# Row-wise infinity norm of an 8192 x 8192 matrix: a tiled load-and-reduce loop replaced by a ring with hand-placed semaphores, 64 KB runs, a shrinking tail and a split first load

## The chip, the cores and the metric

The kernel runs on one core of one Trainium2 chip. The metric is the device time of one execution in microseconds (us); the program is one launch, with its input and its output in the chip's main memory.

## The reference

For every row of `x`, the largest absolute value in the row:

```
x: float32, 8192 rows x 8192 columns
out[i] = max over j of |x[i, j]|          # np.linalg.norm(x, ord=np.inf, axis=1)
```

So 268.44 MB are read, and 8192 numbers (32 KB) are written. There is no reuse of data.

## The kernel before

The 8192 rows are cut into T = 64 tiles of 128 rows; row p of a tile lies in partition p. One tile is 128 x 8192 float32, 4 MB, and one partition's share of it is one run of 32 KB of memory.

A single loop runs over the 64 tiles. For each tile a buffer of a pool of five (`pool`, `bufs=5`) is taken, and the tile is loaded and reduced in pieces of columns. The list `chunks` gives the pieces: 54 tiles have one piece of 8192 columns; the last ten follow the list `COOLDOWN`: seven of 4096 + 4096, then 4096 + 2048 + 2048, then four times 2048, then 2048, 2048, 1536, 1280 and 1280. For each piece:

- L55 issues the load from SyncE (SP), the only engine that issues loads. SP's program is a plain list, so the loads enter its DMA queue in the order of the loop. A load of a tile whose buffer was in use waits, on SP, for the reduce that read that buffer five tiles before.
- L59 reduces the piece on VectorE (DVE) along the columns with `max` of absolute values. For a tile of one piece the result goes to column t of `res` (128 x 64), else to a column of `partial`.
- For a tile of several pieces, L68 then reduces the few columns of `partial` to column t of `res`. It has to wait for the reduce just before it on the same engine.

After the loop, L78 transposes `res` on TensorE (PE) with an identity matrix that GpSimd (POOL) made at the start, L80 copies the 64 x 128 result from PSUM to SBUF on VectorE, and L81 stores it from SP, 64 rows of 512 B. The tile framework places all semaphores. It ends with a barrier of all engines, a clearing of semaphores and a second barrier.

So the order of the work is: SP's list of loads, held back only by free buffers; VectorE's list of reduces, held back by landings; and a last chain of transpose, copy, store and barriers after the last reduce.

Of the kernel before, what the change touches and what calls it, by code (L numbers as in the profile page):

```python
# [1 line left out]

# [5 lines left out]


COOLDOWN = (
    [[4096, 4096]] * 7
    + [[4096, 2048, 2048]]
    + [[2048, 2048, 2048, 2048]]
    + [[2048, 2048, 1536, 1280, 1280]]
)


@with_exitstack
def kernel(  # L20
    ctx: ExitStack,
    tc: tile.TileContext,
    x: bass.AP,
    out: bass.AP,
):
    nc = tc.nc
    P = 128
    n_rows, n_cols = x.shape
    assert n_rows % P == 0

    T = n_rows // P
    if n_cols == 8192 and T >= len(COOLDOWN):
        chunks = [[n_cols]] * (T - len(COOLDOWN)) + COOLDOWN
    else:
        chunks = [[n_cols]] * T

    x_t = x.rearrange("(t p) m -> t p m", p=P)

    pool = ctx.enter_context(tc.tile_pool(name="sbuf", bufs=5))
    single = ctx.enter_context(tc.tile_pool(name="single", bufs=1))  # L40
    psum_pool = ctx.enter_context(tc.tile_pool(name="psum", bufs=1, space=bass.MemoryType.PSUM))

    res = single.tile([P, T], mybir.dt.float32)
    maxch = max(len(c) for c in chunks)
    if maxch > 1:
        partial = single.tile([P, maxch], mybir.dt.float32)

    for t in range(T):
        ch = chunks[t]
        assert sum(ch) == n_cols  # L50
        xt = pool.tile([P, n_cols], x.dtype)
        off = 0
        for h, w in enumerate(ch):
            dst = res[:, t : t + 1] if len(ch) == 1 else partial[:, h : h + 1]
            nc.sync.dma_start(  # L55
                out=xt[:, off : off + w],
                in_=x_t[t, :, off : off + w],
            )
            nc.vector.tensor_reduce(  # L59
                out=dst,  # L60
                in_=xt[:, off : off + w],
                axis=mybir.AxisListType.X,
                op=mybir.AluOpType.max,
                apply_absolute_value=True,
            )
            off += w
        if len(ch) > 1:
            nc.vector.tensor_reduce(  # L68
                out=res[:, t : t + 1],
                in_=partial[:, : len(ch)],  # L70
                axis=mybir.AxisListType.X,
                op=mybir.AluOpType.max,
            )

    ident = single.tile([P, P], mybir.dt.float32)
    make_identity(nc, ident)
    res_t_psum = psum_pool.tile([T, P], mybir.dt.float32)
    nc.tensor.transpose(res_t_psum, res, ident)  # L78
    res_t = single.tile([T, P], mybir.dt.float32)
    nc.vector.tensor_copy(out=res_t, in_=res_t_psum)  # L80
    nc.sync.dma_start(out=out.rearrange("(t p) -> t p", p=P), in_=res_t)  # L81


# [1 line left out]
_INS = ['x']  # L85
_OUTS = [((8192,), 'float32')]


# [23 lines left out]
```

## Time and profile before

| What | Value |
|---|---|
| time, median of 3 runs | 634.72 us (634.71 to 634.74) |
| the profiled execution's own time | not listed apart from the three |
| span of the profiled execution, first to last instruction | 632.9 us |
| VectorE busy | 558.9 us, 88%, 91 instructions |
| PE busy | 0.4 us |
| GpSimd busy | 0.7 us |
| input loads | 80, in one DMA queue |
| reduces of 8192 columns (L59) | 54, mean 8686 ns |
| reduces of 4096 / 2048 columns (L59) | 15 at 4416 ns / 8 at 2278 ns |
| second reduce of a cut tile (L68) | 10, mean 156 ns |
| PE transpose (L78), copy (L80) | 393 ns, 283 ns |
| issue of a full load to its landing, median | 39.8 us |
| store of the result, issue to landing | 1.8 us |

How to read the profile: the page cuts the span into 40 slices of 15.8 us. The DMA row is the mean busy share of the core's 16 DMA engines in each slice, in tenths, and the GB/s row is what they moved. The chain that ended last is followed back from the last instruction, at each step to what released it. A line of the timeline gives the start in us, the length in us, the engine, the source line, the operation with output<-input, the shapes, how many instructions are merged in it, and in brackets the idle time before it and what ended that. A line of the window table gives a stretch in us, its length, the busy time of PE, PE's weight load, VectorE and GpSimd with numbers of instructions, the granted clock, the DMA engines' busy share and the GB/s they moved.

### The profile page before, as it was taken

How to read it: one execution, taken by the hardware profiler on the slowest of the kernel's cores; microseconds unless marked ns; L12 is line 12 of the kernel's file. 1: busy time of each engine (PE TensorE's matmuls, PEld its weight loads, DVE VectorE, ACT ScalarE, POOL GpSimd, SP SyncE). 2: the span in 40 equal slices, each digit the busy share in tenths (PEclk: the TensorE clock that was granted, in tenths of full speed). 3: DMA queues.
4: the chain of work that ended last, by engine and by line, in shares of the span. 5: the costliest groups of instructions: out<-in, count | busy, mean ns of one | idle time of the engine just before them, and what ended most of it. 6: DMA issues, size and time to landing. Idle time of an engine off the chain costs nothing.

```text
span 632.9 us, 294 instructions
## 1 busy us (share of the span) xinstructions
PE 0.4 (0%) x1; PEld 0.1 (0%) x1; DVE 558.9 (88%) x91; POOL 0.7 (0%) x6
## 2 busy tenths in 40 slices
PE   0000000000000000000000000000000000000000
PEld 0000000000000000000000000000000000000000
DVE  1988988988989889889898898898988989999997
POOL 0000000000000000000000000000000000000000
DMA  8999999999999999999999999999999999999995
GB/s 373 439 437 437 433 431 433 431 431 431 431 431 431 431 431 431 431 431 431 431 431 431 431 431 431 431 431 431 431 437 433 435 435 418 427 428 431 425 421 219
DMA packets 11602, 268.49 MB, mean 424 GB/s; under 512 B 1296, under 2 KB 1360, under 8 KB 1744
## 3 DMA queue, kind: packets, MB, share of 16 engines
q1 hardware_dynamic: 11600, 268.47, 98.9%
q14 instruction: 2, 0.02, 0.0%
HBM read 268.44 MB, written 0.03 MB: 424 GB/s over the span
## 4 chain that ended last, share of the span: by engine, by line
DMA 75%; DVE 24%; SPq 0%; issue 0%; PE 0%; DVEq 0%
DMA xt<-in_x_dram 75%; DVE res L59 15%; DVE partial L59 8%; SPq L55 0%; DVE res L68 0%; PE res_t_psum L78 0%; DVE res_t L80 0%; DVEq L59 0%
## 5 line engine op out<-in xcount | busy, mean ns | idle before, releaser
L59 DVE TENSOR_REDUCE res<-xt 128x1 f32<-128x8192 f32 x54 | 469.0, 8686 | 67.6 <-DMA xt<-in_x_dram 67.6
L59 DVE TENSOR_REDUCE partial<-xt 128x1 f32<-128x4096 f32 (+3 forms) x26 | 88.1, 3430 | 2.7 <-DMA xt<-in_x_dram 2.6
L68 DVE TENSOR_REDUCE res<-partial 128x1 f32<-128x2 f32 (+3 forms) x10 | 1.6, 156 | 0.3
L80 DVE COPY res_t<-res_t_psum 64x128 f32<-64x128 f32 x1 | 0.3, 283 | 0.6 <-PE res_t_psum L78 0.6
L78 PE MATMUL res_t_psum<-ident,res 128*64 128x128 f32 x1 | 0.4, 393 | 629.5 <-DVE res L68 629.5
masks.py:199 POOL TENSOR_SCALAR_AFFINE_SELECT ident<-ident 128x128 f32<-128x128 f32 x1 | 0.3, 292 | 0.1
L78 PEld LDWEIGHTS res_t_psum<-ident,res 128*64 128x64 f32 x1 | 0.1, 128 | 629.4 <-issue 629.4
masks.py:197 POOL MEMSET ident<- 128x128 f32 x1 | 0.2, 204 | 0.3 <-POOLq L96 0.3
L96 POOL MEMSET const-bfloat16-1.0<- 128x1 bf16 x1 | 0.1, 101 | 0.0
L96 POOL MEMSET const-uint8-127<- 128x1 uint8 x1 | 0.1, 101 | 0.0
L96 POOL MEMSET const-float32-0.0<- 128x1 f32 x1 | 0.1, 98 | 0.2 <-issue 0.2
L96 POOL MEMSET const-float32-1.0<- 128x1 f32 x1 | 0.1, 98 | 0.0
## 6 DMA issues: line engine op xcount, KB each, us to landing
xt<-in_x_dram SPq DMA_DIRECT2D x54, 4096.0 KB, 39.8
xt<-in_x_dram SPq DMA_DIRECT2D x15, 2048.0 KB, 38.7
xt<-in_x_dram SPq DMA_DIRECT2D x8, 1024.0 KB, 28.3
xt<-in_x_dram SPq DMA_DIRECT2D x2, 640.0 KB, 17.9
xt<-in_x_dram SPq DMA_DIRECT2D x1, 768.0 KB, 19.3
out_dram<-res_t SPq DMA_DIRECT2D x1, 32.0 KB, 1.8
```

What stands on the lines that cost most here:

```text
L59: nc.vector.tensor_reduce(out=dst, in_=xt[:, off : off + w], axis=mybir.AxisListType.X, op=mybir.AluOpType.max, apply_absolute_value=True,)
L68: nc.vector.tensor_reduce(out=res[:, t : t + 1], in_=partial[:, : len(ch)], axis=mybir.AxisListType.X, op=mybir.AluOpType.max,)
L78: nc.tensor.transpose(res_t_psum, res, ident)
L80: nc.vector.tensor_copy(out=res_t, in_=res_t_psum)
L96: nc = _bacc.Bacc("TRN2", target_bir_lowering=False, num_devices=1)
```

## The change

The loop over tiles is replaced by a list of `pieces` and a critical block (`tc.tile_critical`) in which every wait and every increment of a semaphore is written by hand.

- *64 KB runs.* The first 6144 rows are cut into 24 blocks of 256 rows. A partition takes two rows that follow each other in memory (`R = 2`), one run of 64 KB; a load is 128 x 16384 columns, 8 MB, and one reduce with a three-dimensional input gives two results per partition.
- *Ring.* The five buffers become one tile of 3 x 16384 columns (`RING`). `Ring.take` gives the pieces their places in turn and notes the last earlier piece that used the place; the load waits on SP for that piece's reduce (semaphore `reduced`).
- *Shrinking tail.* The last 2048 rows are 16 tiles of 128 rows. `tail_pieces` works out their pieces backwards from a last one of 640 columns, from a cost of a load and a cost of a reduce written in the program. The widths are: nine tiles of 8192; three of 4096 + 4096; 4160 + 4032; 2624 + 2624 + 2944; 2176 + 2176 + 2048 + 1792; 1344 + 1408 + 1216 + 1088 + 960 + 832 + 704 + 640. With the blocks that makes 56 pieces.
- *No second reduce.* The partial results of a cut tile are written into the ring right behind the place of its last piece, and the last piece's reduce takes them in. Before it VectorE waits for its own preceding reduce.
- *First load split.* The first piece is loaded by two DMAs, partitions 0 to 15 and partitions 16 to 127, on one semaphore.
- *Results.* The results of the 24 blocks are transposed on PE (two transposes), copied on ScalarE (ACT) and stored from ACT's queue while the tail is still loading; those of 15 tail tiles likewise before the end. The last tile's 128 results are turned by a 32 x 32 block transpose on VectorE and stored by SP, 4 rows of 128 B.
- GpSimd waits for the three stores and clears the semaphores at the end of the block.

The core of the diff:

```diff
-    for t in range(T):
-        ch = chunks[t]
-        xt = pool.tile([P, n_cols], x.dtype)
...
-            nc.sync.dma_start(out=xt[:, off : off + w], in_=x_t[t, :, off : off + w])
-            nc.vector.tensor_reduce(out=dst, in_=xt[:, off : off + w], ...)
...
-    nc.tensor.transpose(res_t_psum, res, ident)
-    nc.vector.tensor_copy(out=res_t, in_=res_t_psum)
-    nc.sync.dma_start(out=out.rearrange("(t p) -> t p", p=P), in_=res_t)
+    x_big = x[:split].rearrange("(t p r) m -> t p (r m)", p=P, r=R)
+    x_tail = x[split:].rearrange("(t p) m -> t p m", p=P)
...
+    ring = single.tile([P, RING + PAD], f32)
...
+    with tc.tile_critical(name="norm", no_gpsimd_drain=True):
...
+        for i, (p, sem) in enumerate(zip(pieces, loaded)):
+            dst = ring[:, p["at"] : p["at"] + p["w"]]
+            for a, b in ((0, ENGINES), (ENGINES, P)) if i == 0 else ((0, P),):
+                load = nc.sync.dma_start(out=dst[a:b], in_=p["src"][a:b])
+                if p["before"] >= 0:
+                    load.wait_op(reduced, p["before"] + 1, "sem-ge")
+                load.then_inc(sem, 16)
+        nc.vector.memset(last, 0.0)
+        for i, (p, sem) in enumerate(zip(pieces, loaded)):
+            if p["behind"]:
+                nc.vector.wait_ge(reduced, i)
+            elif p["after"] >= 0:
+                nc.vector.wait_ge(reduced, p["after"] + 1)
+            src = ring[:, p["at"] : p["at"] + p["w"] + p["behind"]]
+            nc.vector.tensor_reduce(
+                out=p["dst"],
+                in_=src.rearrange("p (r m) -> p r m", r=p["rows"]),
+                axis=mybir.AxisListType.X,
+                op=mybir.AluOpType.max,
+                apply_absolute_value=True,
+            ).wait_op(sem, 16 if i else 32, "sem-ge").then_inc(reduced, 1)
+        nc.vector.transpose(out=last_t, in_=last).wait_op(
+            reduced, len(pieces), "sem-ge"
+        ).then_inc(reduced, 1)
...
+        nc.tensor.wait_ge(reduced, n_big)
+        for r in range(R):
+            nc.tensor.transpose(ps[r], res_big[:, :, r], ident).then_inc(turned, 1)
+        nc.tensor.wait_ge(reduced, n_before_last)
+        nc.tensor.transpose(ps_tail, res_tail[:, : n_tail - 1], ident).then_inc(turned, 1)
...
+        nc.sync.dma_start(
+            out=out_tail[n_tail - 1].rearrange("(b k) -> b k", k=32),
+            in_=last_t.rearrange("(b c) k -> c b k", c=32)[0],
+        ).wait_op(reduced, len(pieces) + 1, "sem-ge").then_inc(stored, 16)
+        nc.gpsimd.wait_ge(stored, 48)
+        nc.clear_and_free_semaphores([*loaded, reduced, turned, copied, made, stored])
```

The program of `tail_pieces`, which sets the widths:

```diff
+LOAD = (1.1775e-3, 0.075)
+REDUCE = (1.0417e-3, 0.060)
+FIRST = 640
+GRAIN = 64
+def tail_pieces(n_cols, big):
+    slack = 0.0
+    lag = REDUCE[0] * FIRST + REDUCE[1]
+    rows = []
+    while True:
+        left, row = n_cols, []
+        while left:
+            w = FIRST if not rows and not row else int((lag + slack - REDUCE[1]) / REDUCE[0])
+            w = max(GRAIN, w // GRAIN * GRAIN)
+            if w >= left:
+                w = left
+            elif 2 * w > left:
+                w = (left // 2 + GRAIN - 1) // GRAIN * GRAIN
+            row.append(w)
+            left -= w
+            slack += (LOAD[0] - REDUCE[0]) * w + LOAD[1] - REDUCE[1]
+        rows.append(row[::-1])
+        if (lag + slack - REDUCE[1]) / REDUCE[0] > big:
+            return rows[::-1]
```

## The prediction

> **What bounds the kernel now.** I read the page's busy slices first, then the chain that ended last, then the groups with shapes kept apart, then the timeline of the end. From the page:
>
> ```profile
> DMA  8999999999999999999999999999999999999995
> GB/s 373 439 437 437 433 431 433 431 431 431 431 431 431 431 431 431 431 431 431 431 431 431 431 431 431 431 431 431 431 437 433 435 435 418 427 428 431 425 421 219
> DMA packets 11602, 268.49 MB, mean 424 GB/s; under 512 B 1296, under 2 KB 1360, under 8 KB 1744
> q1 hardware_dynamic: 11600, 268.47, 98.9%
> DMA 75%; DVE 24%; SPq 0%; issue 0%; PE 0%; DVEq 0%
> ```
>
> The 16 DMA engines are full from the second slice to the last but one at one flat rate, 431 GB/s. VectorE's share of the chain misleads: the chain steps through a reduce because a load waits for a buffer, while three more loads stand queued. So the stream of 268.4 MB sets the time, plus what precedes its first byte and follows its last. Those ends, from the timeline:
>
> ```profile
> 12.88 8.69 DVE L59 TENSOR_REDUCE res<-xt 128x1 f32<-128x8192 f32 x1 [12.88 <-DMA xt<-in_x_dram]
> ...
> 602.09 8.81 DVE L59 TENSOR_REDUCE partial<-xt 128x1 f32<-128x4096 f32 x3 [0.35 <-DMA xt<-in_x_dram]
> 610.92 0.16 DVE L68 TENSOR_REDUCE res<-partial 128x1 f32<-128x3 f32 x1
> 611.12 8.86 DVE L59 TENSOR_REDUCE partial<-xt 128x1 f32<-128x2048 f32 x4
> 620.02 0.16 DVE L68 TENSOR_REDUCE res<-partial 128x1 f32<-128x4 f32 x1
> 620.21 8.92 DVE L59 TENSOR_REDUCE partial<-xt 128x1 f32<-128x2048 f32 x5
> 629.17 0.16 DVE L68 TENSOR_REDUCE res<-partial 128x1 f32<-128x5 f32 x1
> ```
>
> From 602.09 VectorE no longer waits for data; it runs back to back to 629.3. The window table shows when the bytes stop:
>
> ```profile
> 624.00:625.00 1.00, 0.00 (x0) 0.00 (x0) 1.00 (x2) 0.00 (x0) 1.00 1.02 415
> 625.00:626.00 1.00, 0.00 (x0) 0.00 (x0) 1.00 (x1) 0.00 (x0) 1.00 0.27 108
> 626.00:627.00 1.00, 0.00 (x0) 0.00 (x0) 1.00 (x2) 0.00 (x0) 1.00 0.03 10
> ```
>
> Most engines end near 625.4, the slowest at 626.4 (last packet record). So VectorE finishes 2.9 us after the last byte.
>
> [...]
>
> **The change, part by part.** The profiled execution's own time is not listed beside its span of 632.87 us; the three runs span 634.71 to 634.74, so I take 634.72 for it and carry the 1.85 us outside the span unchanged.
>
> *Longer runs, fewer loads.* Full-width landings come 9.714 us apart (48.57 per five in the chain, 41.98 to 90.55); pairs of 4096 take 9.79 (reduce starts 572.71, 582.50, 592.30). A load of n columns thus costs 0.076 + 0.0011766 n us. There are 80 input loads before, and 57 after, the extra half of the first not counted as a saving: 24 fewer x 0.076 = -1.8. If a 64 KB run is carried as two packets of 32 KB, only the 9 ns completion packet of each load goes: -0.2. I take -1.8, since each load's packets have grown in one piece with the row so far (6912 = 54 x 128 packets of 32 KB in the records).
>
> *Ring instead of five buffers.* Three slots of 16384 columns. A load takes 19.35 (0.076 + 16384 x 0.0011766), its reduce 17.22 (16384/960 + 0.153, the fixed part from 8686 ns for 8192 columns). Load i+3 waits for reduce i, which ends 2.1 us before load i+1 lands; load i+2 is still whole in the queue. Cost 0, hidden by 21 us of queued data; only SP's later loads stand behind that wait, in their order anyway. All tail waits, taken through the ring the same way, are met over 30 us before their bytes are due.
>
> *Tail.* The program makes 9 single rows and 7 cut ones, 32 pieces, ending in 640 columns. Back-to-back reduces cost n/960 + 0.060 (2.193 between starts at 2048 columns). A cut row waits for its own last partial: 0.035 + 0.093 instead of a second reduce (before 0.19). VectorE last waits for data at piece 32, the last 8192. The last byte, seen 0.5 us late by VectorE (completion packet to reduce start, before), moves from 626.9 to 625.1; behind piece 32 remain 57344 columns and 23 loads, 69.2 us, so it is seen at 555.9. From there 65536 columns 68.3 + 24 x 0.060 + 7 x 0.13 + 0.1 = 70.7: reduces end at 626.6 instead of 629.3, -2.7 with the -1.8 inside it, so -0.9 of its own. VectorE stays the last at the end by 0.7 (625.1 + 0.83 for the last piece is 625.9).
>
> *Last step.* Before: end of the last reduce to the store's issue, 629.32 to 630.21, 0.89 (PE, copy, two handovers). After: a 32x32-block transpose on VectorE, not in the trace; from 0.16 (the tiny reduces) to 0.28 (the copy), take 0.19, + 0.06 of handover: 0.25. -0.64. The other results leave earlier through PE and ACT: 24 x 1 KB and 15 x 512 B packets inside the stream, under 0.2 us on any DMA engine; the 15-row chain (0.4 + 0.3 + 1.8) lies under the last row's 8.9 us.
>
> *Barriers.* The critical block adds one handover before the loads and one round with a semaphore clear at the end. Before, the first issue is at 0.74 after one such handover and the two closing rounds take 0.79 in all. So +0.2 and +0.5, bounds +0.3 to +1.2. SP's loads stand behind the first, all engines behind the second.
>
> *First load split.* Before, the engines' first packets start between 1.76 and 2.59 us, [...] with 16 rows first, all could start at once. Gain at most 0.6, take 0.3, if nothing else changes. But those 16 runs of 64 KB go to partitions 0 to 15. A run takes 2.41 us [...] (16384 x 0.0011766 / 8). [...] 4 x 2.41 = 9.6 [...] +7.2 over 2.41. Then 112 rows, 7 per engine; I take consecutive rows, 16+7e to 22+7e for engine e. [...] Stepping the 16 queues in order, [...] the last engine has done its eight runs after 36.2 us, against 8 x 2.41 = 19.3: +16.9. Nothing gives it back: the stream is full from there on. [...] I take +16.9.
>
> Sum: 634.72 - 1.8 - 0.9 - 0.64 + 0.7 + 16.9 = 649.0.
>
> **Rivals.** [...] -0.3 stands for the split: 631.8, with the barrier and packet bounds 630.5 to 633.5. For it: the saving at both ends is plain in the timeline, [...] The sign turns at a split cost of 2.6 us. *Only the first MiB suffers.* [...] 631.8 + 0.3 + 7.2 = 639.3. *Dealt in turn:* 689. *64 KB runs do not exist as packets:* 1.6 back, [...] within 0.2 to 0.3% of no change.
>
> **How the numbers follow.** [...] blocks of seven 0.42, first MiB only 0.12, dealt in turn 0.04: slower 0.58. Faster 0.39 (near 631.8), within 0.2% 0.03; 0.2% (1.3 us) is about what a measurement of this kernel can tell from no change. The likeliest case alone spans 646 to 652. As both signs hold much of the chance, the range runs from 630.5 to 652; what it leaves out is the turn-dealt case and the edges.
>
> **What would show it.** [...] the first reduce starts near 39 (2.6 start + 36.2 + 0.5), the first slice of GB/s stays under 200, then 431 and above. Without it: the first reduce near 22 (twice the data of before, where it was 12.88), 373 or more in the first slice. Landings 19.35 apart in the middle show the packet term; the last reduce ending under 1.6 us after the last byte shows the tail; transpose to store issue 0.25 the last step; more than 0.8 from landing to the end of the span the barrier. I am wrong if the 16-row load's packets take 2.4 us each.

## The result and the profile after

The changed kernel takes 654.05 us (median of 4 runs, 653.55 to 654.43) against 634.72 (634.66 to 634.74): ratio 1.0305, 95% interval 1.0290 to 1.0319, slower by 19.3 us. The profiled execution took 653.82 us, its span is 651.9. The forecast sign, slower, holds; the forecast size, 649.0 with an upper end of 652, was 5 us too small.

From the page of the changed kernel, the rows that were shown of the kernel before:

```profile
DMA  9989999999999999999999999999999999999995
GB/s 157 277 273 442 446 410 438 442 446 406 434 450 442 406 438 450 438 406 442 446 430 418 442 446 410 438 442 446 406 432 428 440 426 426 440 417 429 424 419 216
DMA packets 8155, 268.48 MB, mean 412 GB/s; under 512 B 947, under 2 KB 986, under 8 KB 2138
q1 hardware_dynamic: 8088, 268.44, 98.7%
DMA 57%; DVE 37%; issue 5%; another core or an unknown queue 1%; SPq 0%; DVEq 0%
```

Two rows contradict each other in the first three slices: the DMA engines are "busy" at 9 tenths and more, yet move 157, 277 and 273 GB/s instead of 430 and more. The engines hold packets that take long: the first sixteen 7.7 to 9.2 us each, where a packet of the later blocks takes 2.42. From the fourth slice on the stream is as full as before. (The rates count whole packets, so how many packets of 2.4 us fall into a slice makes them swing, here between 406 and 450.) The timeline of the start and of the end of the same kernel:

```profile
44.60 17.22 DVE L163 TENSOR_REDUCE res_big<-ring 128x2 f32<-128x16384 f32 x1 [43.49 <-DMA ring<-in_x_dram]
63.84 17.22 DVE L163 TENSOR_REDUCE res_big<-ring 128x2 f32<-128x16384 f32 x1 [2.02 <-DMA ring<-in_x_dram]
...
637.31 2.02 DVE L163 TENSOR_REDUCE res_tail<-ring 128x1 f32<-128x1795 f32 x1 [0.50 <-DVE ring L163]
639.25 8.37 DVE L163 TENSOR_REDUCE ring<-ring 128x1 f32<-128x1344 f32 x7
...
647.72 0.83 DVE L163 TENSOR_REDUCE last<-ring 128x1 f32<-128x647 f32 x1
648.58 0.21 DVE L170 STREAM_TRANSPOSE last_t<-last 128x32 f32<-128x32 f32 x1
648.82 0.66 SPq L209 DMA_DIRECT2D out_dram<-last_t  x1
```

The first block's reduce starts at 44.6 us; the second's 19.2 us later, close to the undisturbed pace of 19.35. All of the loss lies ahead of the first reduce. At the end stand seven reduces, the last, the transpose and the store, with no wait for data between them; ahead of them VectorE stands still once for 0.50 us, which the last part takes up.

### The profile page after: what moved, and what is told of

It reads as the page before. It is cut to its first block, busy times and chain, and to the rows that moved or that the text cites. A ratio compares the mean times of both kernels' runs of the same rounds, so it can differ in the third digit from the quotient of the medians.

```text
span 651.9 us, 206 instructions
## 1 busy us (share of the span) xinstructions
PE 1.0 (0%) x3; PEld 0.2 (0%) x3; DVE 552.9 (85%) x58; ACT 2.0 (0%) x4; POOL 0.7 (0%) x6
## 4 chain that ended last, share of the span: by engine, by line
DMA 57%; DVE 37%; issue 5%; another core or an unknown queue 1%; SPq 0%; DVEq 0%
DMA ring<-in_x_dram 57%; DVE res_big L163 26%; DVE ring L163 6%; DVE res_tail L163 4%; DVE last L163 0%; SPq L150 0%; DVE last_t L170 0%; DVEq L159 0%; SPq L239 0%; SPq L137 0%
## 5 line engine op out<-in xcount | busy, mean ns | idle before, releaser
L163 DVE TENSOR_REDUCE res_big<-ring 128x2 f32<-128x16384 f32 x24 | 413.3, 17220 | 92.4 <-DMA ring<-in_x_dram 92.4
L163 DVE TENSOR_REDUCE res_tail<-ring 128x1 f32<-128x8192 f32 (+4 forms) x15 | 100.5, 6731 | 2.4 <-DMA ring<-in_x_dram 1.3
L163 DVE TENSOR_REDUCE ring<-ring 128x1 f32<-128x4096 f32 (+11 forms) x16 | 38.7, 2463 | 0.0
```

The source lines that it names most:

```text
L163: nc.vector.tensor_reduce(out=p["dst"], in_=src.rearrange("p (r m) -> p r m", r=p["rows"]), axis=mybir.AxisListType.X, op=mybir.AluOpType.max,
```

## The experiments

A time with a number of runs is a median; the others are of one run each. The kernel before took 634.58 to 634.76 us beside them. "Packet" is one 64 KB run of one DMA engine, read from the packet records of the trace; in a kernel without trouble it takes 2.42 us. Sixteen packets are under way at a time. The records do not name the engine, so a "round" here is 16 packets in the order of their ends. The diffs leave out one more edit: the number of increments for which the first block's reduce waits, 16 for each of its DMAs.

**The split undone.** In the loop over loads:

```diff
-            for a, b in ((0, ENGINES), (ENGINES, P)) if i == 0 else ((0, P),):
+            for a, b in ((0, P),):
```

> The changed kernel with one edit undone: the first block is loaded by one DMA of 128 rows. [...] the first reduce starts near 22.3 us (2.4 start, 19.4 load, 0.5) instead of 44.6, every 64 KB packet takes 2.42 us from the first on, and the time is 654.0 - 21.5 = 632.5, faster than the kernel before by 0.3 to 0.5%. Rival, the 64 KB runs or the ring cost most of the loss: first packets stay far over 2.42 us and the time stays above 640. Prediction's own sum without the split's cost: 631.8.

Measured: 632.29 us (632.00 to 632.67, 5 runs), ratio to the kernel before 0.9960, interval 0.9946 to 0.9975: 0.4% faster than the kernel before, and 3.3% faster than the changed one. Its first two large reduces, from the timeline:

```profile
22.78 17.22 DVE L163 TENSOR_REDUCE res_big<-ring 128x2 f32<-128x16384 f32 x1 [21.67 <-DMA ring<-in_x_dram]
42.10 17.22 DVE L163 TENSOR_REDUCE res_big<-ring 128x2 f32<-128x16384 f32 x1 [2.11 <-DMA ring<-in_x_dram]
```

The first one starts 21.8 us earlier than in the changed kernel, and the whole time is 21.8 us shorter: one line of the diff carries all of the loss. The window tables of the two kernels over the same stretch show it at the DMA engines (last two columns: busy share, GB/s). First the changed kernel, then the one without the split (whole packets are counted here too, so a stretch of 7 or 8 us can be off by a round):

```profile
2.00:10.00 8.00, 0.00 (x0) 0.00 (x0) 0.00 (x0) 0.19 (x1) 0.00 (x0) 1.00 1.13 147
18.00:26.00 8.00, 0.00 (x0) 0.00 (x0) 0.00 (x0) 0.00 (x0) 0.00 (x0) 1.00 0.88 262
26.00:34.00 8.00, 0.00 (x0) 0.00 (x0) 0.00 (x0) 0.00 (x0) 0.00 (x0) 1.00 1.14 262
```

```profile
2.00:10.00 8.00, 0.00 (x0) 0.00 (x0) 0.00 (x0) 0.19 (x1) 0.00 (x0) 1.00 0.97 401
18.00:26.00 8.00, 0.00 (x0) 0.00 (x0) 3.22 (x1) 0.00 (x0) 0.00 (x0) 1.00 0.91 393
26.00:34.00 8.00, 0.00 (x0) 0.00 (x0) 8.00 (x1) 0.00 (x0) 0.00 (x0) 1.00 0.93 401
```

**Where the split stands.** Only `i == 0` becomes `i == 10` (and the sum of 32 is awaited there).

> The changed kernel with the split moved from the first block to the eleventh, in the middle of the full stream. [...] the same 16 and 112 rows cost the stream the same 20 to 22 us wherever they stand, nothing hides it, time 652 to 655, with a hole in the GB/s row near 215 us. Rival, a startup effect (cold queues, first descriptors): no loss, about 632.

Measured: 655.21 us, 0.2 above what was expected. The hole moved with the split; from the page:

```profile
GB/s 385 449 445 389 449 449 449 385 449 449 449 385 193 253 317 449 401 437 445 449 405 433 445 449 409 429 445 449 409 427 421 443 423 439 425 424 426 425 421 204
```

Slices 13 to 15 (196 to 245 us) carry the loss, and the reduce of that block waits 24.2 us. The startup rival falls: nothing about the beginning makes these two DMAs slow.

**Main memory or SBUF.** The first DMA reads other rows, and writes the same partitions:

```diff
-                load = nc.sync.dma_start(out=dst[a:b], in_=p["src"][a:b])
+                load = nc.sync.dma_start(out=dst[a:b], in_=p["src"][0:P:8] if b == ENGINES else p["src"][a:b])
```

> The changed kernel, its first DMA of 16 rows reading every eighth row of the block (512 KB apart in memory) instead of 16 neighbouring ones; still to partitions 0 to 15. Some rows of the first 256 are read twice and others not at all, so their results are not the reference's; bytes and packets are the same. [...] nothing changes, first packets 7.7 to 9.3 us, time 653 to 655. Rival, main memory: the first packets fall towards 2.4 us and 6 us come back.

Measured: 653.43 us, within the expected range, first packets 7.7 to 9.2 us as before. The other way round, eight DMAs read 16 neighbouring rows each and write every eighth partition:

```diff
-            for a, b in ((0, ENGINES), (ENGINES, P)) if i == 0 else ((0, P),):
-                load = nc.sync.dma_start(out=dst[a:b], in_=p["src"][a:b])
+            for k in (0, 4, 1, 5, 2, 6, 3, 7) if i == 0 else (-1,):
+                if k >= 0:
+                    load = nc.sync.dma_start(out=dst[k:P:8], in_=p["src"][16 * k : 16 * k + 16])
+                else:
+                    load = nc.sync.dma_start(out=dst, in_=p["src"])
```

> The changed kernel, its first block loaded by eight DMAs of 16 rows, each to every eighth partition (0, 8, 16, ...), 16 neighbouring rows of memory each; the first 256 results come out in another order than the reference's. [...] packets of 4.5 to 5.1 us from the first on, not 8.5, and 8 x 5.1 = 41 for the block: about 654 to 655. Rival, sixteen rows are slow for their number: first packets 8 us and more and a time above 670.

Measured: 652.43 us, 1.6 under the expected range; first packets 4.2 to 5.6, then about 4.92 in every round. Whether the rows of memory are neighbours or every eighth did not matter (654.05 against 653.43 us), and sixteen rows are not slow for their number (first packets 7.7 to 9.2 us on partitions 0 to 15, 4.2 to 5.6 on every eighth); the partitions decide. Eight rounds of 4.92 are 39.4 us, where eight of 2.42 are 19.4.

**Half of the partitions, two ways.** The first block split at 64; then partitions 32 to 95 first, with 0 to 31 and 96 to 127 behind:

```diff
-            for a, b in ((0, ENGINES), (ENGINES, P)) if i == 0 else ((0, P),):
+            for a, b in ((0, 64), (64, P)) if i == 0 else ((0, P),):
```

```diff
-            for a, b in ((0, ENGINES), (ENGINES, P)) if i == 0 else ((0, P),):
+            for a, b in ((32, 96), (0, 32), (96, P)) if i == 0 else ((0, P),):
```

> The changed kernel with the first block split at partition 64 instead of 16: two DMAs of 64 rows, [...] eight runs per engine at half rate, 8 x 4.8 = 38.6, so the first reduce starts near 41.5 and the time is 19 us above the unsplit one, about 651 to 652. [...] Rival, main memory (the engines collide because they read neighbouring rows): [...] packets 2.4 us, about 632. Rival, a narrow DMA at the start is slow for its shape alone: a quarter of the damage or less, since the DMA is four times as wide.

> The changed kernel, its first block loaded by three DMAs: partitions 32 to 95 first, then 0 to 31, then 96 to 127. [...] the first DMA is as narrow as the 64 rows of the earlier split, [...] its packets take 2.4 us, not 5.1; [...] four packets per engine at up to 5.1, so 5 to 11 us are lost in all, time 637 to 643. Rival, narrowness (fewer than 128 rows is slow whatever the partitions): first packets near 5.1 and a loss of 20 us, 652.

Measured: split at 64, 653.68 us, 1.7 over the expected 652; first round 4.4 to 5.5, the others of the block 4.9 to 5.1. Partitions 32 to 95 first, 643.49 us, 0.5 over its range: 2.5 to 3.3 in the first round (the same as without any split, where it is 2.4 to 3.3), then 2.42 three times, and 4.3 to 5.1 in the four rounds of the two 32-row DMAs. The window table over the first rounds, first split at 64, then 32 to 95:

```profile
5.00:12.00 7.00, 0.00 (x0) 0.00 (x0) 0.00 (x0) 0.00 (x0) 0.00 (x0) 1.00 0.82 169
```

```profile
5.00:12.00 7.00, 0.00 (x0) 0.00 (x0) 0.00 (x0) 0.00 (x0) 0.00 (x0) 1.00 1.04 449
```

Two DMAs of 64 rows each, the same bytes, 16 packets under way in both: 169 against 449 GB/s. (By the packets themselves, 16 x 64 KB in 5.12 or in 2.42 us, it is 205 against 433.) This decides against narrowness: which 64 partitions are written sets the pace. How the rows are dealt to the engines is not shown, since the records name neither the engine nor the partition.

**How far from 32 to 95.** These runs ask for the size. The first DMA takes 64 neighbouring partitions that start at 28, 24, 20 or 16; the rest of the block follows in two DMAs. Counted in steps of four partitions down from 32, they stand one, two, three and four steps away. Two outcomes are set against each other: some packets take about 5 us and the others keep 2.42, or the others are held up with them ("coupled engines"); in steps, the thresholds of the last expectation are two and four. The edit is the same list of (a, b), for example:

```diff
+            for a, b in ((28, 92), (0, 28), (92, P)) if i == 0 else ((0, P),):
```

> The changed kernel, its first block loaded by three DMAs: partitions 16 to 79 first, then 0 to 15, then 80 to 127. [...] of the first 64 packets half take 2.4 us and half 4.8 to 5.1. Theory of coupled engines [...]: all 64 take about the same, 4 to 5 us. This is to tell why the loss was 21.7 us and not the 16.9 [...] Time not told apart, 645 to 656.

> The changed kernel, its first block loaded by three DMAs: partitions 28 to 91 first, then 0 to 27, then 92 to 127. [...] 2 of 16 engines take 4.8 to 5.1 us a packet, 14 take 2.4, four packets long. Coupled engines: the 14 are held up too, to 3 us or more [...] and to 5 if the coupling is full. The time is not told apart, [...] over 645.

> As the run with partitions 28 to 91 first, but the first DMA goes to partitions 24 to 87 (then 0 to 23, then 88 to 127): [...] the 14 others kept 2.42 us a packet; [...] all 16 engines took 5.11. [...] 4 of 16 packets near 5, 12 at 2.42. [...] all 16 at 4.4 to 5.1. The time is not told apart.

> As before with partitions 20 to 83 first (then 0 to 19, then 84 to 127): [...] 6 of 16 packets near 5, 10 at 2.42. [...] the 10 others between 2.42 and 5.1; a threshold at two: all at 5.1; a threshold at four: the 10 others at 2.42. The time is not told apart.

The packets of the second round, when all engines are under way:

| first partitions | steps from 32 | packets, second round |
|---|---|---|
| 32 to 95 | 0 | 16 at 2.42 |
| 28 to 91 | 1 | 14 at 2.42, 2 at 5.0 |
| 24 to 87 | 2 | 16 at 5.2 |
| 20 to 83 | 3 | 16 at 5.1 |
| 16 to 79 | 4 | 16 at 5.1 |

At one step two packets are slow and 14 keep their pace. From two steps on, all 16 are slow. Of the expected outcomes, the threshold at two came true. These four runs do not tell whether the number of steps decides or which partitions are written, since each takes four lower partitions beside those of the run before it. The window table over 5 to 12 us at one step, then at two:

```profile
5.00:12.00 7.00, 0.00 (x0) 0.00 (x0) 0.00 (x0) 0.00 (x0) 0.00 (x0) 1.00 1.00 412
```

```profile
5.00:12.00 7.00, 0.00 (x0) 0.00 (x0) 0.00 (x0) 0.00 (x0) 0.00 (x0) 1.00 0.88 178
```

The whole times of these four, 667.93 (start at 16), 664.35 (28), 672.71 (24) and 673.32 (20), are not for comparison: the two DMAs for the rest of the block differ from run to run in their rows and partitions. The expected 645 to 656 of the first was a miss; in its last DMA, 48 rows to partitions 80 to 127, every packet took 8.0 to 8.5 us.

**The other parts.** On the kernel without the split: large blocks loaded as two DMAs of 32 KB runs; the old widths of the tail; and the first block split along its columns.

```diff
-            for a, b in ((0, ENGINES), (ENGINES, P)) if i == 0 else ((0, P),):
-                load = nc.sync.dma_start(out=dst[a:b], in_=p["src"][a:b])
+            n = p["rows"]
+            for a in range(n):
+                c = slice(a * n_cols, (a + 1) * n_cols) if n > 1 else slice(0, p["w"])
+                load = nc.sync.dma_start(out=dst[:, c], in_=p["src"][:, c])
```

```diff
-    tail = tail_pieces(n_cols, R * n_cols)
+    tail = (
+        [[8192]] * 6
+        + [[4096, 4096]] * 7
+        + [[4096, 2048, 2048]]
+        + [[2048, 2048, 2048, 2048]]
+        + [[2048, 2048, 1536, 1280, 1280]]
+    )
```

```diff
-            for a, b in ((0, ENGINES), (ENGINES, P)) if i == 0 else ((0, P),):
-                load = nc.sync.dma_start(out=dst[a:b], in_=p["src"][a:b])
+            for a, b in ((0, 1024), (1024, 2 * n_cols)) if i == 0 else ((0, p["w"]),):
+                load = nc.sync.dma_start(out=dst[:, a:b], in_=p["src"][:, a:b])
```

> The unsplit kernel with each of its 24 large blocks loaded by two DMAs with runs of 32 KB, into the same place and reduced as before; only run length and number of loads differ. Prediction's term: a load costs 0.076 us beside its bytes, 24 loads more give +1.8, about 634.1. Rival, only the completion packets count (9 ns a load): +0.2, about 632.5.

> The unsplit kernel with the widths of the tail taken from the kernel before (six tiles of 8192, seven of 4096 + 4096, then 4096 + 2048 + 2048, four times 2048, and 2048, 2048, 1536, 1280, 1280); the number of pieces stays 32. Prediction's term for the shrinking tail: +0.9, about 633.2, the last reduce ending some 2 to 3 us after the last byte. Rival, the tail's shape is worth nothing since VectorE is the last in both: within 0.3 of 632.3.

> The unsplit kernel with its first block split along the columns: 128 rows x 1024 columns, then 128 rows x 15360. [...] one load more, +0.08, and no earlier start, [...] 632.2 to 632.6, the same as the unsplit kernel. Rival, any split of the first load costs (two DMAs on one semaphore, more issue work): 633 or more.

Measured: runs of 32 KB, 633.91 us (633.68 to 634.50, 20 runs; ratio to the kernel before 0.9989, 0.9982 to 0.9995), 1.6 more than with 64 KB, near the expected 634.1. Old tail, 632.80 (632.55 to 633.46, 10 runs; 0.9970, 0.9961 to 0.9979): 0.5 more, between the two outcomes expected, and the intervals overlap, so this is no more than likely. In its profile the last reduce ends 2.6 us after the last byte, against 2.05 with the new widths and no split. Split along columns, 632.78 (632.73 to 632.87, 6 runs; 0.9968, 0.9956 to 0.9981): 0.2 over the expected range, with an interval that overlaps that of the unsplit kernel. Its first large reduce starts at 23.48, no earlier than without a split. It gains nothing, and at the medians it costs 0.5 us where the split by rows costs 21.8.

## Why the prediction was right or wrong

Right in the sign and in the cause that it named, too small in the size by one assumption.

| Step | Predicted | Measured | From |
|---|---|---|---|
| longer runs, fewer loads | -1.8 | -1.6 | 32 KB against 64 KB runs |
| tail | -0.9 | -0.5, not clear of the scatter | old against new widths |
| last reduce's end to the store's issue, 0.89 before | -0.64 (0.25) | -0.62 (0.27) | timeline, 648.55 to 648.82 |
| first issue later | +0.2 | +0.21 | 0.95 against 0.74 |
| store's issue to the end of the span | +0.5 | +0.4 | 3.08 against 2.66 |
| sum without the split's cost | 632.1 (631.8 with a gain of 0.3) | 632.29 | split undone |
| the split | +16.9 | +21.8 | split kept against undone |

- *What bounds it.* The stream, as said: a hole in it, at the start or in the middle, comes out in full in the time (21.8 and 22.9 us). The ring's waits hid as planned: in the changed kernel, from the second block on, large reduces start 19.35 us apart. The tail fell short: a cut row's wait was put at 0.13 us, but one took 0.50 (the line at 637.31 above; its bytes had landed at 635.44). The kernel without the split has the same stop. What VectorE waited for there is not shown.
- *The failed step* is the term "the last engine has done its eight runs after 36.2 us". It was the author's estimate, and no trace of before shows what went into it: a quarter of the pace for the 16 rows (4 x 2.41 = 9.6), and for the 112 rows that some engines go on at 2.41 us a run however long the others take. From the first packet's start to the last one's end the block took 41.5 us. The first round was right, 9.5 us where the estimate was 9.6; the other seven took 32.0 instead of 26.6. The packet records of the changed kernel, round by round (smallest to largest, us):

```
round     1          2          3          4          5          6          7          8
packets   7.7-9.2    5.2-6.4    4.6-4.9    2.9-4.8    3.5-4.7    4.1-4.7    4.6-4.8    4.5-4.8
```

In round 4, 14 packets take 2.9 to 3.3 and just two take 4.8; in round 5, 14 take 3.5 to 3.6 and two 4.4 and 4.7. That is like one step above, two slow packets beside 14 faster ones. That these 14 do not reach 2.42 fits engines out of step: when the fast packets of round 4 have ended, its other two are under way for another 2.2 us, beside the first of round 5; an estimate from these records, 2.2 us at half pace and the rest of the packet at full pace, gives 3.5. In the five other rounds after the first, all 16 packets take 4.1 us or more, as from two steps on above. So what failed is that engines go on at 2.41 beside held-up ones: 14 packets did at one step, and none in these rounds. Whether the 112 rows were dealt in blocks of seven is not shown. The median rounds sum to about 39 us where a free engine of the prediction had 26.5 (9.6 + 7 x 2.41); round 9, the next block's first, still takes 2.6 to 3.7 instead of 2.42. The first reduce was expected near 39 and came at 44.6.
- *Other sums and signs of the prediction.* "The first slice of GB/s stays under 200, then 431 and above" does not follow from its own 36.2 us, which reach into the third slice of 15.8; the second and third moved 277 and 273 GB/s. "The last reduce ending under 1.6 us after the last byte" does not follow from its sum either: 626.6 less the last packet's end, 626.4 - 1.8, is 2.0. Without the split it was 2.05, in the changed kernel 2.9, the same as before the change. And for the rival at 631.8, 630.5 to 633.5 do not come out of its terms: the barrier's bounds give 631.4 to 632.3, the packet term up to 633.9. That the sum without the split came within 0.2 us of 632.29 is in part luck, since its terms were off by up to 0.4 each.
- *The rivals.* The one at 631.8, faster since the split costs nothing, fell: undoing the split gave back 21.8 us. "Only the first MiB suffers" fell: rounds 2 to 8 lose more than round 1. "Dealt in turn" was put at 689 and fell with the measured 654.05. "64 KB runs do not exist as packets" fell: 3072 packets of 65536 bytes, at 2.42 us.
- *Chances.* The 0.39 for a faster kernel rested in part on the old stream, in which the packets hardly differ: of its 6912 packets of 32 KB, 99 in 100 took at most 1.222 us, with a median of 1.218. That trace could not have shown what narrower loads do, since all of its loads are 128 rows wide. The range failed at its upper end of 652, which left the 36.2 us almost no room above themselves; it should have held the case that the slowest queue holds up all the others. In the prediction's own terms that is 9.6 us for the first round and 2 x 2.41 for each of seven more, 43.4 in all, seven above its 36.2.

What stays open: why packets take twice as long when some sets of partitions are written and not when others are, and why 14 packets keep their 2.42 us beside two of 5.0 at one step while all 16 are slow from two steps on. No run here shows it.

## What to carry to other kernels

For a large DMA into SBUF, look at which partitions it covers: all 128, or 32 to 95, kept 2.42 us a packet here; 0 to 63, every eighth and the stretches of 64 from 24, 20 and 16 took about twice that, 0 to 15 over three times. Where a load has to be cut into pieces, cut it along the columns: at 632.78 against 632.29 us that cost nothing clear of the scatter here, while every cut along the partitions that was tried cost 11 us or more (it started nothing earlier, though, since the reduce waits for the whole block). A DMA row at 9 tenths beside a falling GB/s row was here the sign of packets that took two to four times their 2.42 us. And price every part of a bundled change by itself: here the other parts were worth 2.4 us together, and one line cost 21.8.

## What the runs showed of the hardware

- With the first DMA on partitions 32 to 95, 16 packets take 2.42 us; on 28 to 91, 14 take 2.42 and two 5.0; on 24 to 87, 20 to 83 and 16 to 79, all 16 take 5.1 to 5.2 (second round, one run each).
- Where every round is alike (partitions 0 to 63, every eighth), a packet takes 4.9 to 5.2 us, up to 7% over twice 2.42 (4.84). In the changed kernel, where the rounds differ, every packet took 4.1 to 4.9 in rounds 3 and 6 to 8. On partitions 0 to 15 a packet took 7.7 to 9.2.
- From the last completion packet of a full load to the start of its reduce: 0.36 us at the first tile of the kernel before, rising to 0.5 later on; 0.35 to 0.5 in the kernel without the split; 1.1 us at the first block of the changed kernel and about 0.57 at the others.
- In the kernel before, two fetches of 8 KB of instructions took 0.32 us each. Right behind each, one data packet took 0.41 and 0.66 us longer than its fellows.
